# A first projection by Strassen's identity in a hybrid decoder layer, with every engine's instructions in program order

## The chip, the cores and the metric

The kernel runs on one core of one Trainium2 chip. The metric is the time of one execution in microseconds (us) of device time. Of the kernel before there are three timed runs, with a median of 2120.15 us (2118.58 to 2121.61), and one profiled execution.

## What is computed

The layer takes x of 1024 tokens by 2048, all in float32. It normalises x, scales and shifts it by a modulation computed from c, and projects the result h to 8192 columns. These hold eight quantities of eight heads with 128 columns each: q, k, v, z of a stick-breaking attention, and q, k, v, z of a retention. The two groups' outputs are gated with SiLU(z), joined, projected back with `w_out`, gated and added to x.

```python
mod = silu(c) @ w_ada + b_ada
shift, scale, gate = split(mod, 3)
h = rms_norm(x, norm_gain) * (1.0 + scale) + shift          # 1024 x 2048
proj = h @ w_in                                             # 2048 x 8192, the "first projection"
q_sb, k_sb, v_sb, z_sb, q_r, k_r, v_r, z_r = split(proj)    # 1024 columns each, 8 heads of 128
qa, ka = rms_norm(q_sb, sb_q_gain), rms_norm(k_sb, sb_k_gain)          # per head
# stick-breaking, per head: z = qa.ka / sqrt(128); for s < t
#   A[t,s] = sigmoid(z[t,s]) * prod_{s<j<t} (1 - sigmoid(z[t,j]));  oa = A @ v
oa = stick_breaking_attention(qa, ka, v_sb) * silu(z_sb)
# retention, per head: o_t = sum_{s<=t} gamma^(t-s) (q_t.k_s) v_s, in chunks of 128 with a state
ob = head_group_norm(chunkwise_retention(rotary(q_r), rotary(k_r) / sqrt(128), v_r)) * silu(z_r)
y = concat(oa, ob) @ w_out                                  # 2048 x 2048, the "second projection"
return x + gate * y
```

## The kernel before

**Numbers and products.** Every large product is made in a split form: a float32 operand is cut into a high part and a low part (both in the type fp32r), and three matmuls, high by high, high by low and low by high, are added up in PSUM. `mm3` (L130 to L134) issues the three. A weight tile that has arrived from memory is cut by `split_w`: ScalarE (ACT) copies the high part (`wh`, L118), and VectorE (DVE) subtracts it to get the low part (`wl`, L120). The activations h are kept whole on chip for the entire first projection, 16 row chunks of 128 by two token halves of 512, as `h_hi` and `h_lo`.

**First projection.** Two helpers compute it. `unit_t` makes one head of one quantity transposed (128 columns by 512 tokens): the weights are the stationary operand, h is the moving one. `unit_v` makes two heads of v with the tokens on the partitions: h is stationary and 256 columns of weights move.

```python
def unit_t(col0, halves, name, lo_pool=()):          # 16 chunks x 2 halves x 3 matmuls of 512 columns
    ...
            mm3(o[hf], hi[:, sl], lo[:, sl], h_hi[kc, hf], h_lo[kc, hf], kc == 0, kc == KC - 1)
def unit_v(col0, name):                              # 16 chunks x 8 token blocks x 3 matmuls of 256 columns
    ...
            mm3(o[tb // 2][:, (tb % 2) * 256:(tb % 2) * 256 + 256],
                h_hi[kc, tb // 4][:, tk], h_lo[kc, tb // 4][:, tk], hi[:, sl], lo[:, sl], ...)
```

**Stages.** (1) Start: x is loaded, normalised and turned; the modulation is summed from `w_ada` chunk by chunk (`ada_sums`, two-pass float32 matmuls `accp`, L282); meanwhile the z columns of seven retention heads are computed for the first token half, as chunks of h become ready (`first`), before the shift is known. Then the other token half of these columns, while the shift is summed and added to h (`shift_h`, L318 to L323); the missing share of the shift is added to z later (`z_bias`). (2) For each stick-breaking head: q, k, z by `unit_t`, and for every second head v by `unit_v`. In between, the attention of the head before is issued piece by piece. (3) The same for the retention heads. (4) The second projection, in output columns of 512: first the two token halves of the first columns (`y_0a`, `y_0b`), then three units with all eight token blocks (`y`).

**Order.** TensorE (PE) runs in the order in which the program issues: after every six matmuls of a projection, `tick` lets one waiting task (a generator such as `sb_attention`, `ret_attention`, `qk_norm`, `gate_parts`) issue its next piece. The other engines' order is chosen by the tile layer's scheduler, with some steps raised by `high_priority`. Buffers are tags of tile pools.

**Queries and keys.** `qk_norm` squares q and k on GpSimd (POOL), averages over the head by a matmul with a constant matrix (`ms`, L545 and L546), and takes the inverse root on tiles of 128x512 by three Newton steps on ACT and DVE (L553 to L555). z and v of a head go to memory (`zsb`, `vraw`) and come back when the attention needs them.

**End.** `finish` (L944 to L948) loads a tile of x (`xr`), multiplies the projection's tile by the gate, adds x, and stores.

Of the kernel before, what the change touches and what calls it, by code (L numbers as in the profile page):

```python
# [11 lines left out]
F32 = mybir.dt.float32  # L12
# [5 lines left out]
P = 128  # L18
S = 1024
# [11 lines left out]
NORM_GAP = 3  # L31
NORM_GAP2 = 6
SPLIT_GAP = 2
ZT = 1
BE = 3
TURN = 2
TURN_PRIO = 400
RT_ONE = False
ZB_GAP = 2
K0_WAIT = 8  # L40
NZ = 7
ADA_BUFS = 9
SHIFT_GAP = 6
X_LOAD = {3: (4,), 5: (5,), 7: (6,), 8: (7,)}
X_STAT = {5: (4,), 7: (5,), 9: (6,), 10: (7,)}
X_TURN = 10
MOD_AT = 4
ENG = mybir.EngineType
MANUAL = (ENG.PE,)
LO_POOL = ()  # L50
RT_GAP = 5
# [3 lines left out]
def layer_kernel(ctx, tc, x, c, w_ada, b_ada, norm_gain, w_in, sb_q_gain, sb_k_gain, ret_norm_gain, w_out,  # L55
# [7 lines left out]
    hp = ctx.enter_context(tc.tile_pool(name="hp", bufs=1))  # L63
    wp = ctx.enter_context(tc.tile_pool(name="wp", bufs=3))
    ps = ctx.enter_context(tc.tile_pool(name="ps", bufs=1, space=PS))
    dr = ctx.enter_context(tc.tile_pool(name="dr", bufs=1, space=bass.MemoryType.DRAM))

    concat = [dr.tile([P, S], F32, name=f"concat{f}") for f in range(KC)]
    gate_row = dr.tile([1, D], F32, name="gate_row")

# [5 lines left out]
    mean_r = cons.tile([P, P], F32R, name="mean_r")  # L76
    nc.vector.memset(mean_r.bitcast(F32), 1.0 / HD)

    c_sb = hp.tile([P, HALF], F32, tag="hl14_1", name="c_sb")[:, 0:16]
# [9 lines left out]
    rows = hp.tile([P, HALF], F32, tag="hl15_1", name="rows")  # L89
# [8 lines left out]
    nc.vector.tensor_copy(cols, rows_ps[:, 0:58])  # L98
    gain_c = cols[:, 0:16]
    shift_b = cols[:, 16:32]  # L100
    qg = cons.tile([P, 1], F32, name="qg")
    nc.vector.tensor_scalar(qg, cols[:, 48:49], 1.0 / math.sqrt(HD), None, op0=ALU.mult)
    kg = cols[:, 49:50]
# [9 lines left out]


    def split_w(raw, name, lo_eng=nc.vector):
        n = raw.shape[1]
        hi = wp.tile([P, HALF], F32R, tag="wh", name=f"wh_{name}")
        nc.scalar.activation(hi[:, 0:n], raw, AF.Copy)  # L118
        lo = wp.tile([P, HALF], F32R, tag="wl", name=f"wl_{name}")
        lo_eng.tensor_tensor(lo[:, 0:n], raw, hi[:, 0:n].bitcast(F32), op=ALU.subtract)  # L120
        return hi, lo

    def wchunk(parts, name, lo_eng=nc.vector):
        raw = wp.tile([P, HALF], F32, tag="wr", bufs=3, name=f"wr_{name}")
        for dst, src in parts(raw):
            nc.sync.dma_start(dst, src)
        return split_w(raw, name, lo_eng)

    w_in_k = w_in[0].rearrange("(k p) n -> p k n", p=P)

    def mm3(o, a_hi, a_lo, b_hi, b_lo, first, last):
        nc.tensor.matmul(o, a_hi, b_hi, start=first, stop=False)  # L132
        nc.tensor.matmul(o, a_hi, b_lo, start=False, stop=False)  # L133
        nc.tensor.matmul(o, a_lo, b_hi, start=False, stop=last)  # L134
# [3 lines left out]
    def unit_t(col0, halves, name, lo_pool=()):  # L138

        o = {hf: ps.tile([P, HALF], F32, tag="pj", bufs=4, name=f"pj_{name}_{hf}") for hf in halves}  # L140
        for kq in range(4):
            def parts(raw):
                yield raw.rearrange("p (k n) -> p k n", n=P), w_in_k[:, 4 * kq:4 * kq + 4, col0:col0 + P]
            with tc.high_priority(AHEAD):
                hi, lo = wchunk(parts, f"{name}_{kq}", nc.gpsimd if kq in lo_pool else nc.vector)
            for hf in halves:
                for k in range(4):
                    kc = 4 * kq + k
                    sl = slice(k * P, (k + 1) * P)
                    mm3(o[hf], hi[:, sl], lo[:, sl], h_hi[kc, hf], h_lo[kc, hf], kc == 0, kc == KC - 1)  # L150
                    if k % 2:
                        yield
        return o

    def unit_v(col0, name):

        o = [ps.tile([P, HALF], F32, tag="pj", bufs=4, name=f"pv_{name}_{b}") for b in range(4)]
        for kk in range(8):
            def parts(raw):
                yield raw.rearrange("p (k n) -> p k n", n=2 * P), w_in_k[:, 2 * kk:2 * kk + 2, col0:col0 + 2 * P]  # L160
            with tc.high_priority(AHEAD):
                hi, lo = wchunk(parts, f"{name}_{kk}")
            for tb in range(NB):
                for k in range(2):
                    kc = 2 * kk + k
                    sl = slice(k * 2 * P, (k + 1) * 2 * P)
                    tk = slice(tb % 4 * P, (tb % 4 + 1) * P)
                    mm3(o[tb // 2][:, (tb % 2) * 256:(tb % 2) * 256 + 256],
                        h_hi[kc, tb // 4][:, tk], h_lo[kc, tb // 4][:, tk], hi[:, sl], lo[:, sl],
                        kc == 0 and tb % 2 == 0, kc == KC - 1 and tb % 2 == 1)  # L170
                if tb % 2:
                    yield
        return o
# [3 lines left out]
    tasks = []  # L177
    one_step = [True]

    def tick():  # L180
        stepped = False
        for task in list(tasks):
            task[1] -= 1
            if task[1] > 0 or stepped and one_step[0]:
                continue
            stepped = True
            try:
                task[1] = next(task[0])
            except StopIteration:
                tasks.remove(task)  # L190

# [3 lines left out]
    def steady(unit):  # L195
        while True:
            try:
                next(unit)
            except StopIteration as e:
                return e.value  # L200
            tick()

    def drain():
        while tasks:
            tick()
# [5 lines left out]
    zcol = 7 * GW  # L211
    zraw = [dr.tile([P, S], F32, name=f"zraw{h}") for h in range(NZ)]
    shift = cons.tile([P, KC], F32, name="shift")
    zsb = [dr.tile([P, S], F32, name=f"zsb{h}") for h in range(NH)]
    vraw = [dr.tile([P, NB, 2, P], F32, name=f"vraw{i}") for i in range(NH // 2)]
    zb = cons.tile([P, 8], F32, name="zb")
    with tc.tile_pool(name="st", bufs=1) as st:
        xt, ada, xT = {}, {}, {}

        def load_x(t):  # L220
            for qt in range(4):
                xt[t, qt] = hp.tile([P, HALF], F32, tag=f"hh{4 * qt + t % 4}_{t // 4}", name=f"x_{t}_{qt}")
                nc.sync.dma_start(xt[t, qt], x2[t * P:(t + 1) * P, qt * HALF:(qt + 1) * HALF])

        def load_ada(cc, gs=range(4)):

            col = (D if cc < 8 else 0) + (cc % 8) * 2 * P
            for g in gs:
                ada[cc, g] = ar = st.tile([P, 4, 2 * P], F32, tag="ada", bufs=ADA_BUFS, name=f"ada_{cc}_{g}")
                nc.sync.dma_start(ar, ada_rows[:, 4 * g:4 * g + 4, col:col + 2 * P])  # L230

        def half_tile(name):
            return st.tile([P, HALF], F32, tag="ht", bufs=3, name=name)

        def x_squares(ts):
            ss = st.tile([P, 2, 4], F32, tag="ss", bufs=2, name=f"ss_{ts[0]}")
            for i, t in enumerate(ts):
                for qt in range(4):
                    junk = half_tile(f"junk_{t}_{qt}")
                    nc.scalar.activation(junk, xt[t, qt], AF.Square, accum_out=ss[:, i, qt:qt + 1])  # L240
            return ss

        def x_scale(ts, ss):

            n = len(ts)
            nc.vector.tensor_tensor(ss[:, 0:n, 0:2], ss[:, 0:n, 0:2], ss[:, 0:n, 2:4], op=ALU.add)
            m = st.tile([P, 2], F32, tag="m", bufs=2, name=f"m_{ts[0]}")
            nc.vector.tensor_tensor(m[:, 0:n], ss[:, 0:n, 0], ss[:, 0:n, 1], op=ALU.add)
            nc.vector.tensor_scalar(m[:, 0:n], m[:, 0:n], 1.0 / D, EPS, op0=ALU.mult, op1=ALU.add)
            y = st.tile([P, 2], F32, tag="y", bufs=2, name=f"y_{ts[0]}")  # L250
            u = st.tile([P, 2], F32, tag="u", bufs=2, name=f"u_{ts[0]}")
            rsqrt_newton(y[:, 0:n], m[:, 0:n], u[:, 0:n])
            for qt in range(4):
                for i, t in enumerate(ts):
                    if i % 2:
                        nc.scalar.activation(xt[t, qt], xt[t, qt], AF.Copy, scale=y[:, i:i + 1])
                    else:
                        nc.vector.tensor_scalar(xt[t, qt], xt[t, qt], y[:, i:i + 1], None, op0=ALU.mult)

        def x_turn(kc, g, tag, bufs):  # L260

            xT[kc, g] = hp.tile([P, HALF], F32, tag=f"hl{kc}_{g}", name=f"xT{kc}_{g}")
            tp = ps.tile([P, HALF], F32, tag=tag, bufs=bufs, name=f"xtp_{kc}_{g}")
            for t in range(4):
                src = xt[4 * g + t, kc // 4]
                nc.tensor.transpose(tp[:, t * P:(t + 1) * P], src[:, (kc % 4) * P:(kc % 4 + 1) * P], ident)
# [93 lines left out]
        for t in range(4):  # L360
            load_x(t)
# [644 lines left out]
```

## Time and profile before

| | before |
|---|---|
| median of three runs | 2120.15 us |
| the profiled execution: its time, its span | 2122.75 us, 2120.8 us |
| PE / DVE / ACT / POOL busy | 2074.5 / 1117.3 / 701.1 / 202.0 us |
| granted PE clock, mean | 0.999 |
| moved by DMA | 224.31 MB, 106 GB/s on average |

The profile's page gives the busy time of each engine, the same in 40 slices of the span (a digit is tenths), the chain of work that ended last, and groups of instructions. Matmuls overlap each other in the records: a record is longer than the distance to the next one, so costs of matmuls are taken from the distance of their starts. A two-pass float32 matmul (operands not in fp32r) has two records; a transpose has one. SP is the engine that issues nearly all DMA transfers, in order, on one queue.

### The profile page before, as it was taken

The numbers are of one execution on the slowest core, as the hardware profiler recorded it, in microseconds if no ns is written. First come the engines' busy times: TensorE is split into PE (matmuls) and PEld (weight loads), VectorE is DVE, ScalarE is ACT, GpSimd is POOL, SyncE is SP. The second block draws the span as 40 slices with busy tenths as digits, with TensorE's granted clock in tenths as the row PEclk, the third lists the DMA queues.
The fourth block names the chain that finished last, engine by engine and source line by source line (L and its number), as shares of the span: only waits on it lengthen the run. The fifth ranks groups of instructions, "written<-read, shape, count | busy, mean of one in ns | idle before, by whom it ended". The sixth has DMA issues, their size and how long they took to land.

```text
span 2120.8 us, 30239 instructions
## 1 busy us (share of the span) xinstructions
PE 2074.5 (98%) x11679; PEld 1771.8 (84%) x11679; DVE 1117.3 (53%) x2165; ACT 701.1 (33%) x1312; POOL 202.0 (10%) x342
## 2 busy tenths in 40 slices
PE   5999999999999999999999999999999999999998
PEld 4777789888988898889888888988989988688887
DVE  4664662768166826783575556466354156513132
ACT  5453442544244514442453232222122223311110
POOL 0000000111021102110211112011011010000000
PEclk9999999999999999999999999999999999999999
DMA  9977212121212122211222533333332125624132
GB/s 293 335 253 226 85 60 75 46 70 60 80 46 70 45 75 66 70 45 55 85 70 87 175 101 113 110 92 102 101 91 63 50 73 167 215 90 134 48 126 79
DMA packets 232403, 224.31 MB, mean 106 GB/s; under 512 B 12674, under 2 KB 187844, under 8 KB 232260
## 3 DMA queue, kind: packets, MB, share of 16 engines
q1 hardware_dynamic: 231872, 222.36, 33.2%
q8 instruction: 91, 1.49, 0.3%
q14 instruction: 52, 0.43, 0.1%
q10 hardware_dynamic: 388, 0.04, 0.0%
HBM read 194.03 MB, written 28.32 MB: 105 GB/s over the span
## 4 chain that ended last, share of the span: by engine, by line
PE 83%; DVE 8%; DMA 5%; ACT 3%; issue 2%; POOL 0%; SPq 0%; ACTq 0%; DVEq 0%; POOLq 0%
PE y L132 4%; PE y L133 4%; PE y L134 4%; PE pv_v L134 3%; PE pv_v L133 3%; PE pv_v L132 3%; PE pj_rq L132 3%; PE pj_rq L134 3%; PE pj_rq L133 3%; PE pj_q L133 3%; PE pj_rk L132 3%; PE pj_rk L134 3%; PE pj_rk L133 3%; PE pj_q L134 3%; PE pj_q L132 3%; PE pj_z L132 2%
## 5 line engine op out<-in xcount | busy, mean ns | idle before, releaser
L132 PE MATMUL y<-wh_o,c_hi 128*128 128x512 f32 x384 | 149.4, 389 | 0.0
L133 PE MATMUL y<-wl_o,c_hi 128*128 128x512 f32 x384 | 149.4, 389 | 0.0
L134 PE MATMUL y<-wh_o,c_lo 128*128 128x512 f32 x384 | 149.4, 389 | 0.0
L132 PE MATMUL pv_rv<-wh_rv,h_hi 128*128 128x256 f32 x512 | 145.8, 285 | 3.4 <-ACT wh_rv L118 3.4
L133 PE MATMUL pv_rv<-wl_rv,h_hi 128*128 128x256 f32 x512 | 145.3, 284 | 1.8 <-DVE wl_rv L120 1.8
L133 PE MATMUL pv_v<-wl_v,h_hi 128*128 128x256 f32 x512 | 144.9, 283 | 0.0
L132 PE MATMUL pv_v<-wh_v,h_hi 128*128 128x256 f32 x512 | 144.9, 283 | 0.0
L134 PE MATMUL pv_v<-wh_v,h_lo 128*128 128x256 f32 x480 | 135.8, 283 | 0.0
L134 PE MATMUL pv_rv<-wh_rv,h_lo 128*128 128x256 f32 x480 | 135.8, 283 | 0.0
L120 DVE TENSOR_TENSOR wl_o<-wr_o,wh_o 128x512 fp32r<-128x512 f32 x48 | 33.2, 692 | 181.7 <-ACT wh_o L118 181.7
L627 DVE TENSOR_TENSOR_SCAN om<-om 128x128 f32<-128x128 f32 (+2 forms) x96 | 96.3, 1003 | 43.5 <-POOL om L617 42.2
L118 ACT ACTIVATE wh_o<-wr_o 128x512 fp32r<-128x512 f32 x48 | 30.3, 632 | 220.7 <-PE y L134 216.3
L132 PE MATMUL pj_rq<-h_hi,wh_rq 128*128 128x512 f32 x256 | 102.6, 401 | 0.0
L132 PE MATMUL pj_rk<-h_hi,wh_rk 128*128 128x512 f32 x256 | 102.3, 400 | 0.0
L132 PEld LDWEIGHTS pv_rv<-wh_rv,h_hi 128*128 128x128 f32 x512 | 98.2, 192 | 4.9 <-ACT wh_rv L118 4.0
L132 PE MATMUL pj_z<-h_hi,wh_z 128*128 128x512 f32 x256 | 101.3, 396 | 0.0
L133 PEld LDWEIGHTS pv_rv<-wl_rv,h_hi 128*128 128x128 f32 x512 | 98.2, 192 | 2.7 <-DVE wl_rv L120 2.6
L132 PE MATMUL pj_k<-h_hi,wh_k 128*128 128x512 f32 x256 | 100.3, 392 | 0.0
L132 PE MATMUL pj_q<-h_hi,wh_q 128*128 128x512 f32 x256 | 100.1, 391 | 0.0
L134 PE MATMUL pj_rq<-h_hi,wl_rq 128*128 128x512 f32 x256 | 100.0, 391 | 0.0
L134 PE MATMUL pj_rk<-h_hi,wl_rk 128*128 128x512 f32 x256 | 99.9, 390 | 0.0
L134 PE MATMUL pj_q<-h_hi,wl_q 128*128 128x512 f32 x256 | 99.9, 390 | 0.0
(270 smaller groups left out, 5520.3 us busy)
## 6 DMA issues: line engine op xcount, KB each, us to landing
ada<-in_w_ada_dram SPq DMA_DIRECT2D x64, 512.0 KB
gr<-in_w_ada_dram SPq DMA_DIRECT2D x64, 256.0 KB
wr_o<-in_w_out_dram SPq DMA_DIRECT2D x48, 256.0 KB
x<-in_x_dram SPq DMA_DIRECT2D x32, 256.0 KB
wr_rz<-in_w_in_dram SPq DMA_DIRECT2D x32, 256.0 KB
wr_q<-in_w_in_dram SPq DMA_DIRECT2D x32, 256.0 KB
wr_k<-in_w_in_dram SPq DMA_DIRECT2D x32, 256.0 KB
wr_z<-in_w_in_dram SPq DMA_DIRECT2D x32, 256.0 KB
```

Source lines behind the costliest of these rows:

```text
L118: nc.scalar.activation(hi[:, 0:n], raw, AF.Copy)
L120: lo_eng.tensor_tensor(lo[:, 0:n], raw, hi[:, 0:n].bitcast(F32), op=ALU.subtract)
L132: nc.tensor.matmul(o, a_hi, b_hi, start=first, stop=False)
L133: nc.tensor.matmul(o, a_hi, b_lo, start=False, stop=False)
L134: nc.tensor.matmul(o, a_lo, b_hi, start=False, stop=last)
L627: nc.vector.tensor_tensor_scan(rev, rev, rev, init, op0=ALU.mult, op1=ALU.bypass)
```

## The change

**Strassen's identity.** The first projection is done as a block product of two by two: columns of `w_in` in pairs of heads, rows in two halves of 1024 (A11, A12, A21, A22, each 128 columns by 1024 rows), and h in two row halves by two token halves (B11 to B22). Seven products of half size replace eight. On the side of h the seven right factors (B11, B21, B22 and the combinations T1 to T4) are made once, cut into high and low parts, and stored in memory (`fac`, 56 pairs of 256 KB tiles). On the side of the weights the sums and differences are made by DVE on the arrived tiles (`one_sum`, and one subtraction in `left`). Three of the four results accumulate over several products in PSUM and are read in between; the rest is added by DVE (`evac`).

**Groups.** 56 pairs of heads' columns make seven groups of four pairs. A group runs seven products, each over two row quarters (`hh`) and four pairs (`q`): an entry is four chunks, twelve matmuls of 512 columns. For each entry the weights are loaded, summed and cut three entries ahead (`LOOK`), and the right factors come from memory through 24 slots (`ring`). There are 400 entries.

**Plain first.** The columns computed first and without Strassen are now the queries of seven retention heads (both token halves, 672 matmuls of 512); the eighth head's queries ride along in group 0. While the second token half runs, the shift is summed, the right factors are made (`factors`) and mostly stored.

**v and the others.** v is computed transposed like the rest and turned by PE when the attention needs it (`turn_v`, `values_in`); `unit_v` is gone. Every result of a group except the retention z goes to memory (`proj`) and is read back. `qk_norm` is replaced by `prepare`: squares on ACT, sums by `nm` (a two-pass float32 matmul with 32 columns of ones), roots on tiles of 128x16, the inverse root of q as the scale of the two sigmoids, that of k as a row read back on all partitions.

**Order and buffers.** From the second plain pass on, all engines run in program order (`tc.manual_schedule()` without a list). Steps that need another engine's result are issued some ticks later (`later(n, ...)`). All large tiles are 92 slots of 128x512 given out by hand (`Slots`), from a certain point on in classes (14 for results, 24 for raw weights, 24 for the ring, 30 for attention).

**The second projection** keeps its matmuls. The retention z is gated there (`cut_step`), six of the eight gate parts are summed there (`gate_steps`), and the x tiles are loaded two token blocks ahead (`load_xr`).

The core of the diff:

```diff
-ctx.enter_context(tc.manual_schedule(engines={mybir.EngineType.PE}))
+ctx.enter_context(tc.manual_schedule())
...
+KCS = (0, 1, 8, 9, 2, 3, 10, 11, 4, 5, 12, 13, 6, 7, 14, 15)
+RIGHT = {1: "B11", 2: "B21", 3: "B22", 4: "T4", 5: "T1", 6: "T2", 7: "T3"}
+ORDER = (4, 1, 6, 5, 3, 2, 7)
+FRESH = (4, 1, 2, 7)
...
+    for a in range(0, NH, 2):
+        groups.append([(base + a * P, proj[f"{n}{a}"], proj[f"{n}{a + 1}"])
+                       for n, base in (("q", 0), ("k", GW), ("z", 3 * GW), ("v", 2 * GW))])
+    for a in (0, 4):
+        groups.append([(base + b * P, proj[f"{n}{b}"], proj[f"{n}{b + 1}"])
+                       for b in (a, a + 2) for n, base in (("rk", 5 * GW), ("rv", 6 * GW))])
+    groups.append([(7 * GW + a * P, a, a + 1) for a in range(0, NH, 2)])
...
+    def pump():
+        while ring_list and len(slots.free["ring"]) >= 2:
+            gi, prod, kc = ring_list.popleft()
+            n = RIGHT[prod]
+            hi = get(f"{n}h_{gi}_{kc}", "ring", F32R)
+            nc.sync.dma_start(hi.bitcast(F32), fac[n, kc][:, 0])
+            lo = get(f"{n}l_{gi}_{kc}", "ring", F32R)
+            nc.sync.dma_start(lo.bitcast(F32), fac[n, kc][:, 1])
+            ring[gi, prod, kc] = hi, lo
+        n = 2
+        while pumping[0] is True and raw_list and slots.free["raw"] and n:
+            load_raw(*raw_list.popleft())
+            n -= 1
...
+    def one_sum(gi, hh, q, n):
+        r = {b: raws[gi, q, b, hh] for b in ("A11", "A21", "A22")}
+        o, a, b = {1: ("A22", "A22", "A21"), 3: ("A21", "A11", "A21"), 2: ("A11", "A22", "A11")}[n]
+        nc.vector.tensor_tensor(r[o], r[a], r[b], op=ALU.add if n == 1 else ALU.subtract)
...
+    def evac(gi, prod, q, o):
+        def copy(cc):
+            dst[q, cc] = t = get(f"c{cc}_{gi}_{q}", "dst", borrow=gi == LAST)
+            nc.scalar.activation(t, o, AF.Copy)
+        def add(cc):
+            nc.vector.tensor_tensor(dst[q, cc], o, dst[q, cc], op=ALU.add)
...
+    def run_entry(j):
+        gi, prod, hh, q = entries[j]
+        prepare_entry(j + LOOK)
+        if q == 0:
+            for k in range(4):
+                rts[k] = right(gi, prod, 4 * hh + k)
...
+        for k in range(4):
+            sl = slice(k * P, (k + 1) * P)
+            mm3(bank[q], hi[:, sl], lo[:, sl], rts[k][0], rts[k][1], fresh and k == 0, hh == 1 and k == 3, True)
+            if last_q:
+                put(*rts.pop(k))
+            if k == 3 and hh:
+                later(1, lambda: evac(gi, prod, q, o))
+            if k % 2:
+                tick()
...
-    def unit_v(col0, name):
-    def qk_norm(r, gain, pool, name):
+    def prepare(h):
+            nc.tensor.matmul(nm[32 * g:32 * g + 32, 256 * i:256 * i + 256], ones, ...)
```

As built, the instructions change so (counted in the two programs):

| | before | after |
|---|---|---|
| matmuls of 512 columns in the first projection | 4608 | 5472 |
| matmuls of 256 columns in the first projection | 3072 | 0 |
| matmuls of 512 columns in the second projection | 1536 | 1536 |
| matmuls with the constant matrix (`ms`, 512 columns) | 64 | 0 |
| `nm` matmuls, 256 columns, two-pass | 0 | 64 |
| transposes of v and in `prepare` | 0 | 168 |
| DVE / ACT / POOL instructions | 2167 / 1289 / 347 | 2583 / 1378 / 283 |
| DMA transfers, MB | 786, 222 | 1916, 486 |

1724 lines of the change are left out of this document (1043 added, 681 removed).

## The prediction

> **What bounds the kernel now.** I read the page first: busy shares, the 40 slices, the chain.
>
> ```profile
> span 2120.8 us, 30239 instructions
> ...
> PE 2074.5 (98%) x11679; PEld 1771.8 (84%) x11679; DVE 1117.3 (53%) x2165; ACT 701.1 (33%) x1312; POOL 202.0 (10%) x342
> ...
> PE   5999999999999999999999999999999999999998
> ...
> PEclk9999999999999999999999999999999999999999
> DMA  9977212121212122211222533333332125624132
> ...
> q1 hardware_dynamic: 231872, 222.36, 33.2%
> ...
> PE 83%; DVE 8%; DMA 5%; ACT 3%; issue 2%; POOL 0%; SPq 0%; ACTq 0%; DVEq 0%; POOLq 0%
> ```
>
> PE is busy in all slices but the first and is 83% of the chain; the clock is full. But overlapping records make a PE busy that is only slow, so I asked the view of waits what PE waited for (columns: total us, times, longest).
>
> ```profile
> PE accp L282 <- DVE ss L246: 11.0, 1, 11.0
> PE rows_ps L97 <- DMA rows<-in_ret_norm_gain_dram: 8.8, 1, 8.8
> PE pv_rv L132 <- ACT wh_rv L118: 3.4, 3, 2.4
> PE ms_k L545 <- ACT be L615: 3.2, 7, 0.6
> ```
>
> Two waits of the start make 20 us; everything after it is a few us per cause. So the kernel is bound by the number of PE's matmuls, and the question is how many fall away, and whether what replaces them (transfers, DVE sums) stays hidden.
>
> **Prices of PE.** From the timeline, starts (first column) of equal matmuls in a row:
>
> ```profile
> 1930.11 0.39 PE L133 MATMUL y<-wl_o,c_hi 128*128 128x512 f32 x1
> 1935.55 0.39 PE L133 MATMUL y<-wl_o,c_hi 128*128 128x512 f32 x1
> 560.08 0.28 PE L133 MATMUL pv_v<-wl_v,h_hi 128*128 128x256 f32 x1
> 571.00 0.28 PE L134 MATMUL pv_v<-wh_v,h_lo 128*128 128x256 f32 x1
> 28.85 1.95 PE L266 MATMUL xtp<-ident,x 128*128 128x128 f32 x16
> L282 PE MATMUL accp<-ada,silu_z 128*32 128x256 f32 x512 | 33.3, 398 | 12.8 <-DVE ss L246 11.0 <-DMA ada<-in_w_ada_dram 1.1 <-DVE xT L268 0.7
> ```
>
> The two 512-column starts lie 24 matmuls apart: 5.44/24 = 0.227 us each. The 256-column ones lie 91 apart: 10.92/91 = 0.120, so two of them cost 0.240 where one wide one costs 0.227. Sixteen turns take 1.95 us with the last one's length in it: about 0.11 each. The two-pass sums (`accp`) take 33.3/512 = 0.065 a record. All are costs per instruction on the path, since PE hardly waits.
>
> **The sum, against the profiled execution's 2122.75 us** (span 2120.8 and 1.95 around it; 2.6 above the median of the runs, 0.12%).
>
> 1. The 3072 matmuls of `unit_v` go: 3072 x 0.120 = -368.6. The 512-column ones of the first projection go from 4608 to 5472: 864 x 0.227 = +196.1. Net -172.5. Of this, 672 x 0.227 = 152.5 is Strassen's and the rest is v computed wide. Accumulating in PSUM across products adds no matmul.
> 2. `qk_norm`'s `ms` goes: 64 x 0.227 = -14.5. `nm` comes: 64 of two records, 128 x 0.065 = +8.3. 168 turns come: x 0.11 = +18.5. Net +12.3.
> 3. The tail. The chain before ends on a load of x that waited behind PE's end:
>
> ```profile
> 2110.70 0.24 PE y L134
> 2112.41 0.34 SPq L948
> ...
> 2112.81 4.12 DMA xr<-in_x_dram
> ...
> 2117.02 0.69 DVE yt L947
> ```
>
> `load_xr` asks for it two token blocks earlier, so -4 (bounds -4 and 0).
>
> This gives 2122.75 - 172.5 + 12.3 - 4 = 1958.5 if nothing new waits. What could (operations and bytes by stage are counted in the program as built, in its order):
>
> 4. **Transfers.** They grow from 222 to 486 MB. The first matmul of the first projection starts here:
>
> ```profile
> 31.66 0.50 PE L132 MATMUL first<-h_hi,wh_first 128*128 128x512 f32 x1 [0.86 <-ACT h_hi L308]
> ```
>
> With PE's time by the prices above:
>
> | stage | MB | PE us | GB/s asked |
> |---|---|---|---|
> | start and two plain passes | 70 | 32 to that matmul + 200 | 303 |
> | group 0 | 56 | 176 | 321 |
> | groups 1 to 6, each | 49 to 53 | 183 to 198 | 257 to 283 |
> | second projection, first unit | 25 | 90 | 280 |
> | its last three units | 32 | 262 | 122 |
>
> What the engines can move shows where they are full, in the view of windows (last columns: PE clock, DMA share, GB/s):
>
> ```profile
> 0.00:100.00 100.00, 77.98 (x529) 57.46 (x530) 54.77 (x174) 51.30 (x118) 0.70 (x6) 1.00 0.97 323
> 100.00:200.00 100.00, 98.56 (x666) 76.42 (x665) 57.23 (x99) 44.74 (x76) 0.00 (x0) 1.00 0.79 253
> 60.00:100.00 40.00, 40.00 (x251) 30.52 (x250) 26.42 (x93) 17.08 (x42) 0.00 (x0) 1.00 1.05 365
> 1760.00:1868.00 108.00, 104.17 (x457) 82.34 (x456) 60.59 (x125) 35.36 (x57) 1.29 (x1) 0.98 0.62 201
> ```
>
> At a share of 0.97 they moved 323, at best 365; 253 at 0.79 and 201 at 0.62 scale to about 320 full. So groups 1 to 6 ask 80 to 88% of a full rate of 320 or 70 to 78% of 365, with factors asked for two blocks of four entries (20 us and more) ahead: hidden. Up to the end of group 0 it is tight: 126 MB need 391 us at 323 and 346 at 365, beside PE's 32 + 376 = 408. The mean fits; the order within need not, since the store of a factor must end before its slot is loaded again. I take +8, between 0 and +40 (a tenth of the 391). Issuing costs 0.34 of SP's time each (the store above): 1911 x 0.34 = 650 us of some 1980, hidden.
>
> 5. **DVE.** Its 512-element operation costs
>
> ```profile
> L120 DVE TENSOR_TENSOR wl_o<-wr_o,wh_o 128x512 fp32r<-128x512 f32 x48 | 33.2, 692 | 181.7 <-ACT wh_o L118 181.7
> L491 DVE SCALAR_TENSOR_TENSOR ga<-gr,silu_c,ga 128x256 f32<-128x256 f32 x120 | 63.0, 525 | 18.3 <-DMA gr<-in_w_ada_dram 15.8
> 239.56 0.75 DVE L318 SCALAR_TENSOR_TENSOR h<-h_hi,shift,h_lo 128x512 f32<-128x512 f32 x1
> 240.22 0.69 DVE L323 TENSOR_TENSOR h_lo<-h,h_hi 128x512 fp32r<-128x512 f32 x1
> 240.83 0.75 DVE L318 SCALAR_TENSOR_TENSOR h<-h_hi,shift,h_lo 128x512 f32<-128x512 f32 x1
> ```
>
> 0.69 us as a record, and 0.61 to 0.66 from start to start in a dense row. In groups 1 to 5 it has 140 to 150 such operations and 40 to 45 us of small ones: 136 to 147 us beside 183 to 191 of PE, hidden; ACT has 59 to 99 there and POOL less than before. Not hidden are two places. In the second plain pass and the opening of group 0 (weights, bias of the queries, h, and the factors at once) it has 115 operations of 512 and 37 smaller: about 100 us beside 100 of PE, and PE's next entries wait for its `wl`. I take +4 (0 to +12). In the first unit of the second projection it has 116 x 0.69 + 49 x 0.525 = 106 us beside 90: the cuts of the joined outputs, the gating with z moved here, and the gate's sums. By the dense pitch it is 95 to 100. I take +8 (0 to +16).
>
> 6. **Waits from program order.** On DVE, a sum or an `evac` that waits for PE's last matmul of an entry now stands ahead of later `wl` in a fixed queue; PE's entry three further on, 3 x 12 x 0.227 = 8 us later, waits for these. SP's stores stand ahead of factor loads in the same way, covered by the 20 us. With these leads I take what PE already waits now from its third row on, about as much again: +8 (0 to +90, below).
>
> Forecast: 1958.5 + 8 + 4 + 8 + 8 = **1986**; its own range, 1963 to 2015, adds the smaller bounds of 4 to 6.
>
> **Rivals.**
>
> *Nothing new waits: 1958* (1945 to 1963). For it: in groups 1 to 6 no engine is asked for more than PE gives it time for, and the leads of 8 and 20 us exceed the 4.12 us of the load above. Against it: stages at 95 to 100% of a second engine.
>
> *Fixed order costs each block: 2046* (2015 to 2118). A group has 14 blocks (7 products by two row quarters), in all 98; if at each one PE waits about 0.9 us for a `wl` held up behind an `evac`, that is 88 us on 1958. For it: such waits exist already (`pv_rv` for `wh_rv` up to 2.4 us) where DVE and ACT are only half busy. Against it: leads of three entries.
>
> The window of 1760 to 1868 above has PE waits and a clock of 0.98, 2 us lost in 108. [...] No row here shows waits that long outside the start, so this is 1 in 100.
>
> *Transfers become the bound: slower than before.* All go through SP's one queue, and as built eight completion semaphores are used in turn, so a ninth transfer waits for the first. Taking out the last units (262 us, 32 MB) and 22 us at the ends, 454 MB must pass in 2123 - 284 = 1839 us to break even: 247 GB/s. Below that the change loses; at 230 the time is 1974 + 284 = 2258. For it: the run's mean is 106 and no stretch longer than 100 us is over 323; with 512-byte rows in the weights and stores among loads the rate could drop. Against it: the 253 of the second window came at a share of 0.79, so it was the pace asked, not the limit.
>
> The row of 60 to 100 us moved 365 GB/s in transfers of 256 and 512 KB. [...] I give the slower side from transfers 10 in 100.
>
> *The change does not do what it says*: the built program has the 5472 matmuls, so no chance worth a number.
>
> **How the numbers follow.** Forecast 62, nothing waits 12, fixed order 14, slower 11 (10 and 1), no change 1, of 100. What a measurement of this kernel can tell from no change is about 0.2%, 4 us: faster 0.88, same 0.01, slower 0.11. The range takes the first two cases whole and most of the third: 1950 to 2085, leaving out some 3 below and 15 above.
>
> **What would show it.** Right: PE's records about 9,700 (5472 + 1536 wide ones), no slice under 9 but the first, DMA digits of 7 to 9 up to the first unit of the second projection, some 486 MB, DVE near 1300 us; PE's waits of 20 us at the start, then DVE `wl` near 200 us and in the first unit. Wrong: PE digits of 7 or 8 through groups 1 to 6, waits of PE on ring tiles (`T1h`, `B11h`) or on `wl` at every block, a clock under 0.98.

## The result and the profile after

| | before | after |
|---|---|---|
| median of four runs each, same chip | 2120.88 us (2118.58 to 2121.61) | 2053.27 us (2050.84 to 2056.50) |
| ratio of the times | 1 | 0.968, 95% interval 0.967 to 0.970 |
| profiled execution: time, span | 2122.75, 2120.8 us | 2056.50, 2054.8 us |
| granted PE clock, mean | 0.999 | 0.989 |

The change is faster by 67.6 us. The forecast was 135 us faster (1986), so the direction and the range (1950 to 2085) held, and half of the gain did not come. The rest of this document is about the 67 us between 1986 and 2053. One of the four runs of an experiment below (v's load six ticks earlier) took 10989.55 us, so its time is the median of the other three and its trace is not used.

From the page of the kernel after: span, busy times, and the 40 slices of PE, of its clock and of the DMA engines.

```profile
span 2054.8 us, 28414 instructions
...
PE 1944.9 (95%) x9703; PEld 1578.5 (77%) x9703; DVE 1276.4 (62%) x2581; ACT 761.5 (37%) x1401; POOL 81.1 (4%) x278
...
PE   5998899999999999998999999999998998899998
...
PEclk9999899999999999999999999999999999999999
DMA  9967798987686678776866786999987567654041
...
q1 hardware_dynamic: 381194, 485.65, 72.4%
```

9703 records and 485.65 MB are what was forecast, DVE's 1276 us too. New against before are the eights in PE's row: the fourth and fifth slice (154 to 257 us, the second plain pass), single ones later, and a pair at 1695 to 1798 (the second projection's first units). PE has holes there. The view of waits names them (total us, times, longest):

```profile
PE accp L523 <- DVE xT L508: 13.1, 5, 3.2
PE y L186 <- ACT ch L1353: 12.9, 10, 3.0
...
PE zp L186 <- DVE vl L951: 8.0, 6, 1.5
PE otp L1225 <- DVE on L1217: 7.6, 4, 4.2
PE vtp L945 <- DMA vr<-pr_v: 7.4, 4, 2.7
PE zp L186 <- ACT nr L865: 4.7, 4, 1.9
PE rvt L1145 <- DMA rv<-pr_rv: 4.4, 3, 1.8
...
PE pj L187 <- DVE B21l L586: 2.2, 1, 2.2
```

No cause is large, and of those shown only the last, once 2.2 us, is a projection's entry (`pj`) waiting, there for a factor. What waits is not the projection but what is issued between its entries: the modulation's sums (`accp`), v's turns (`vtp`, `rvt`), scores (`zp`), the retention's outputs (`otp`); and, at the end, the first two units of `y`.

To place the loss I put the matmuls of each trace beside the program's order, priced each as in the prediction (0.227, 0.120, 0.11, 0.065 us, and 0.175 for 384 columns), and took for each stage the time from its first matmul's start to that of the next stage, less the priced sum: the time **lost over price**. (The 9 to 10 us ahead of the first matmul of all and the 6 us behind the last one are in no row.)

| us lost over price | before | after |
|---|---|---|
| start, to the first projected matmul | 16.8 | 14.4 |
| the columns done plain (two passes) | 4.0 | 25.3 (1.7 and 23.6) |
| group 0 | | 3.6 |
| groups 1 to 6 (before: the heads) | 32.5 | 83.2 |
| second projection | 11.8 | 32.0 |
| sum | 65.1 | 158.5 |
| priced matmuls, whole kernel | 2041.0 | 1880.3 |

The matmuls are 160.7 us cheaper, as forecast (-172.5 + 12.3 = -160.2). About 93 us came back as holes, where the forecast allowed 28.

**How one hole is made.** In the second plain pass the turned x (`xtp`) leaves PE at 165.7 us and must be copied (`xT`, L508) before PE may write the same PSUM bank again as `accp`. From the timeline of after (start, duration, engine, line, operation), PE first, then DVE:

```profile
165.04 0.66 PE L503 MATMUL xtp<-ident,x 128*128 128x128 f32 x4 [0.28 <-DVE shift L546]
...
170.96 1.93 PE L523 MATMUL accp<-ada,silu_z 128*32 128x256 f32 x32 [3.21 <-DVE xT L508]
```

```profile
165.56 0.68 DVE L573 TENSOR_TENSOR T<-xT,xT 128x512 f32<-128x512 f32 x1
166.16 0.68 DVE L573 TENSOR_TENSOR T<-xT,T 128x512 f32<-128x512 f32 x1
166.76 0.68 DVE L586 TENSOR_TENSOR B21l<-xT,B21h 128x512 fp32r<-128x512 f32 x1
167.36 0.68 DVE L586 TENSOR_TENSOR T1l<-T,T1h 128x512 fp32r<-128x512 f32 x1
167.97 1.15 DVE L175 TENSOR_TENSOR wl_first<-wr,wh_first 128x512 fp32r<-128x512 f32 x2
169.04 1.27 DVE L715 SCALAR_TENSOR_TENSOR qb_acc<-wr,shift,qb_acc 128x512 f32<-128x512 f32 x2
170.23 0.68 DVE L508 COPY xT<-xtp 128x512 f32<-128x512 f32 x1
```

From 165.7 on, the factors (`T`, `B21l`, `T1l`), two weight cuts and two bias sums stand ahead of the one copy that PE needs next. DVE is doing useful work all the while, in the wrong order for PE. PE stands still for 3.21 us. A load does the same on ACT. For the gate of z in the attention, ACT's place for the sigmoid is fixed three ticks after the load is issued; the view of ACT's waits says:

```profile
ACT sg L1043 <- DMA zr<-pr_z: 47.9, 16, 5.1
```

Sixteen times ACT stops for 3.0 us on average, and whatever is queued behind it on ACT is held up by as much.

### The profile page after: what moved, and what is told of

It is laid out like the page before. It is cut to its first block, busy times and chain, and to the rows that moved or that the text cites. A ratio compares the mean times of both kernels' runs of the same rounds, so it can differ in the third digit from the quotient of the medians.

```text
span 2054.8 us, 28414 instructions
## 1 busy us (share of the span) xinstructions
PE 1944.9 (95%) x9703; PEld 1578.5 (77%) x9703; DVE 1276.4 (62%) x2581; ACT 761.5 (37%) x1401; POOL 81.1 (4%) x278
## 3 DMA queue, kind: packets, MB, share of 16 engines
q1 hardware_dynamic: 381194, 485.65, 72.4%
## 4 chain that ended last, share of the span: by engine, by line
PE 69%; DVE 13%; DMA 11%; ACT 3%; issue 3%; SPq 1%; DVEq 0%; ACTq 0%
PE pj L186 13%; PE pj L187 13%; PE pj L188 13%; PE y L186 4%; PE y L187 4%; PE y L188 4%; PE first L186 2%; PE first L187 2%; PE first L188 2%; DMA zr<-pr_z 2%; DVE wl L175 1%; DMA gr<-in_w_ada_dram 1%; PE accp L523 1%; DMA vr<-pr_v 1%; DVE om L983 1%
## 5 line engine op out<-in xcount | busy, mean ns | idle before, releaser
L175 DVE TENSOR_TENSOR wl<-A,wh 128x512 fp32r<-128x512 f32 x400 | 274.4, 688 | 306.7 <-ACT wh L173 277.1
L173 ACT ACTIVATE wh<-A 128x512 fp32r<-128x512 f32 x400 | 251.1, 629 | 458.3 <-PE pj L187 357.6
L186 PE MATMUL y<-wh_o,ch 128*128 128x512 f32 x512 | 203.8, 398 | 12.9 <-ACT ch L1353 12.9
L187 PE MATMUL y<-wl_o,ch 128*128 128x512 f32 x512 | 202.1, 395 | 3.1 <-DVE wl_o L175 3.1
L188 PE MATMUL y<-wh_o,cl 128*128 128x512 f32 x512 | 202.6, 396 | 0.1
L186 PEld LDWEIGHTS y<-wh_o,ch 128*128 128x128 f32 x512 | 97.5, 190 | 38.2 <-ACT ch L1353 17.8
L292 DVE TENSOR_TENSOR A<-A,A 128x512 f32<-128x512 f32 x168 | 113.8, 686 | 9.9 <-DMA A<-in_w_in_dram 8.1
L188 PEld LDWEIGHTS y<-wh_o,cl 128*128 128x128 f32 x512 | 97.4, 190 | 25.7 <-DVE cl L1354 5.6
L187 PEld LDWEIGHTS y<-wl_o,ch 128*128 128x128 f32 x512 | 97.7, 191 | 23.7 <-DVE wl_o L175 3.9
L186 PE MATMUL pj<-T1h,wh 128*128 128x512 f32 x232 | 93.9, 405 | 0.0
```

The costliest lines, as they stand in the source:

```text
L173: nc.scalar.activation(hi[:, 0:n], src[:, 0:n], AF.Copy)
L175: nc.vector.tensor_tensor(lo[:, 0:n], src[:, 0:n], hi[:, 0:n].bitcast(F32), op=ALU.subtract)
L186: nc.tensor.matmul(o, a_hi, b_hi, start=first, stop=False, skip_group_check=on)
L187: nc.tensor.matmul(o, a_hi, b_lo, start=False, stop=False, skip_group_check=on)
L188: nc.tensor.matmul(o, a_lo, b_hi, start=False, stop=last, skip_group_check=on)
L292: nc.vector.tensor_tensor(r[o], r[a], r[b], op=ALU.add if n == 1 else ALU.subtract)
```

## The experiments

Three theories were tried against each other: **order** (pieces stand in the wrong place of a fixed queue, so what PE needs is late although the engines have time), **amount** (DVE has too much to do) and **transfers** (485 MB are too much). A time is the median of four runs unless said otherwise, with the ratio to before on the same chip and its interval; the changed kernel is 2053.27 us, 0.968. The experiments ran on several chips, on which the kernel before took 2120.9 to 2123.2 us, and the intervals are about 3 us either way, so a difference of two times below that is under some 5 us is not clear of noise.

### One hole at a time

*x's copy in the second plain pass, from DVE to ACT.*

```diff
-        if p % 2:
+        if p % 2 and g == 0:
             nc.vector.tensor_copy(xT[kc, g], tp)
```

> In the second plain pass PE lost 23.6 us, half of it where the modulation's sums wait for the PSUM bank that the copy of the turned x on VectorE releases. Here these copies are all made by ScalarE. Order theory (the bank is released late because the copy stands behind the factors' work in VectorE's fixed queue): that wait and the half clock it causes go, the pass shrinks from 123.6 to 102 to 108 us, the whole by 15 to 21 us. Occupancy theory (VectorE has too much work there): 7 copies of 0.69 us move, so at most 5 us. Transfer theory (the DMA engines are full up to the end of group 0): within 4 us of no change.

2055.92 us, 0.969 (0.967 to 0.971): no gain. In its trace the wait for DVE's `xT` is gone and the pass loses 16.1 us over price in place of 23.6, but other waits have come up: `accp` for ACT's `xT` (3.5 us), `xtp` for DVE's `shift` (3.3 for 0.8), and at the opening of group 0, which loses 7.1 for 3.6, `pj` for `wl` (2.5) and ACT's `zt` (1.8). So about half of what the pass gained was lost again at the next place in the fixed queues. The rest went in the unit `y1` (17.4 for 13.5) and group 6 (24.5 for 22.5), far from this edit; runs whose edits change nothing there either lose 15 to 16 and 23 to 25. Neither the 15 to 21 us of the order theory nor the pass of 102 to 108 us (it took 116) came.

*z's gate in the second projection, one chunk ahead.* `gate_z(i + 1)` issues the removed lines for the next chunk after this chunk's cut, so that ACT no longer waits for DVE between `zsg` and `ch`.

```diff
             t = craw.pop((f, half))
-            if f >= NH:
-                z = zkeep.pop((f - NH, half))
-                sg = anywhere(f"zsg_{f}_{half}")
-                nc.scalar.activation(sg, z, AF.Sigmoid)
-                nc.vector.tensor_tensor(z, z, sg, op=ALU.mult)
-                nc.vector.tensor_tensor(t, t, z, op=ALU.mult)
-                put(z, sg)
             hi, lo = anywhere(f"ch_{f}_{half}", F32R), anywhere(f"cl_{f}_{half}", F32R)
...
             c_hi[f, half], c_lo[f, half] = hi, lo
+            gate_z(i + 1)
...
```

> The gating of the retention outputs with SiLU(z) is issued one chunk earlier, behind the cut of the chunk before, with the same instructions. Order theory (ScalarE's cut of the joined outputs waits for a chain ScalarE, VectorE, VectorE and holds up the next weights' cut): the first unit of the second projection shrinks from 120 us to 104 to 108, the whole by 12 to 16. Occupancy theory (VectorE's 106 us of work bound that unit): not below 106, at most 14 and likely under 6, since its work is unchanged. Transfer theory: no change.

2041.97 us, 0.9625 (0.961 to 0.964): 11 us, just under the 12 to 16 expected. The wait of `y` for `ch` falls from 12.9 to 3.0 us, the two units lose 18.9 in place of 30.1, and a wait of 6.1 us for `wl_o` is left.

*v's load six ticks earlier,* and *v's turned copy in another PSUM bank* (A1 in place of A0, which scores and norms share):

```diff
+        vr = {hf: load_v(hf) for hf in range(2)}
         for hf in range(2):
             qt.append(get(f"q_{h}_{hf}", "att"))
...
-            if s == 0:
-                vr = {hf: load_v(hf) for hf in range(2)}
...
```
```diff
-            tp = ps.tile([P, HALF], F32, tag="A0", name=f"vtp_{h}_{hf}")
+            tp = ps.tile([P, HALF], F32, tag="A1", name=f"vtp_{h}_{hf}")
```

> v of a stick-breaking head is asked for six ticks earlier. Transfer theory in its mild form (a load under traffic takes 5 us and more, longer than its five ticks): the waits of the turns of v for that load (7.4 us in all) go, 5 to 8 us less. Order theory: the wait only moves to the next step, within 4 us of no change.

> The turned v uses the PSUM bank A1, which is free then, and no longer A0, which the scores need a tick later. Order theory (short leads on a shared bank): the scores' waits for the low part of v (8.0 us in all) go, 5 to 8 us less. Transfer and occupancy theories: no change.

The early load alone: 2057.31 us over three runs, 0.970 (0.968 to 0.972), nothing. The bank alone: 2045.11 us, 0.9645 (0.963 to 0.966), 8 us; the wait of `zp` for `vl` is gone, and the longest one in the groups is then v's load, 8.1 us in four.

*The last three together:*

> Three edits together: z's gate one chunk ahead (alone -11 us), v's turned copy in the PSUM bank A1 (alone -8 us) and v loaded six ticks earlier (alone nothing). After the bank was changed, TensorE's longest wait in the groups was the one for v's load (8.1 us in four). If leads in series hide one another (the load shows only when the bank is free), the three give 11 + 8 + 5 to 8, about 2026 to 2030 us; if the early load is worth nothing in any case, 2034.

2028.47 us, 0.9555 (0.954 to 0.957), as expected: 25 us, 5 more than the gate and the bank give alone (11 and 8). PE's waits for `vl` and for `vr` are both gone from its list. That fits leads in series, of which the one that ends last hides the others, so that the early load shows only once the bank is free; but 5 us are of the size of the noise (the four runs lie between 2023.65 and 2033.71), so the load's share is not shown by the time alone.

### Amount and transfers

*168 sums of weight blocks left out* (the products take unsummed blocks):

```diff
-        nc.vector.tensor_tensor(r[o], r[a], r[b], op=ALU.add if n == 1 else ALU.subtract)
```

> The 168 sums of weight blocks on VectorE (about 116 us of its 1276) are left out, so that Strassen's products take unsummed blocks; all else stays. If VectorE's amount of work is what holds TensorE back in groups 0 to 6, 25 us or more go, nearly all of them between 256 and 1665 us of the span. If it is the lead of single copies and their place in the order, 5 to 12 us go there, and the second plain pass (23.6 us over its matmuls) and the first two units of the second projection (30 us over) stay within 3 us of what they were.

```profile
PE 1945.3 (95%) x9703; PEld 1578.5 (77%) x9703; DVE 1175.5 (57%) x2413; ACT 761.7 (37%) x1401; POOL 82.1 (4%) x278
```

2052.47 us, 0.966 (0.965 to 0.968). A hundred us of DVE's work are gone and the time is the same within the noise (the intervals of the two ratios overlap); groups 1 to 6 lose 82.5 over price, for 83.2. So the amount of work on DVE was no cause of the groups' holes. The 5 to 12 us that the order theory expected there did not come either.

*The ring loads high parts only* (the low part is left out of the products and the high part stands in):

```diff
-            lo = get(f"{n}l_{gi}_{kc}", "ring", F32R)
-            nc.sync.dma_start(lo.bitcast(F32), fac[n, kc][:, 1])
-            ring[gi, prod, kc] = hi, lo
+            ring[gi, prod, kc] = hi, hi
...
```

> The ring of Strassen's factors loads only their high parts (the low parts are left out of the product, the high part standing in for them), so about 130 MB of the 486 MB are gone and no matmul. If the added time is the price of the transfers (rival: transfers become bound), 25 us or more go, and PE's waits on loads (x, ada, vr, rv: 21 us together) fall by half. If it is short leads in a fixed order, on copies and shared PSUM banks, the time falls by 0 to 6 us, what the waits of vtp for vr (7.4 us) give, and the waits on DVE and ACT stay as they were.

2027.12 us, 0.9546 (0.953 to 0.956): 26 us. Moved were 391.26 MB, so 94 MB fewer and not 130. By the expectation this time speaks for transfers, against the order theory. Groups 1 to 6 lose 52.1 in place of 83.2; the waits for `vr` fall from 7.4 to 2.3 us, ACT's for `zr` from 47.9 to 13.8. The other signs were the order theory's: PE's waits for `xT` (13.0), `ch` (12.8) and `vl` (8.0) stayed, and so did the two loads of the start (18.7). But a late load and a fixed order can't be told apart here; that needs the same cut in a free order (below).

### The order itself

*The one line that fixes all engines.* PE keeps its order; that of the others is chosen by the scheduler.

```diff
-    ctx.enter_context(tc.manual_schedule())
```

> The instruction that fixes every engine to the program's order is taken out; PE's order is still fixed, the others' is chosen by the scheduler, as in the kernel before. If the program's order of VectorE and ScalarE makes the stalls (copies that TensorE needs next stand behind sums, factor openings and gates), the time falls by 15 to 40 us and the waits of accp for xT (13 us) and of y for ch (13 us) go. If TensorE would meet the same short leads whatever the order behind it, it stays within 8 us of the changed kernel or grows, since a scheduler that goes by its own estimate of the times puts other work in front of them.

1972.82 us, 0.929 (0.927 to 0.930): 80 us, twice what was expected at most. The same matmuls, sums and bytes. Page and waits of this kernel:

```profile
PE 1922.8 (98%) x9703; PEld 1579.6 (80%) x9703; DVE 1256.1 (64%) x2581; ACT 766.6 (39%) x1401; POOL 101.0 (5%) x278
...
PE   5999999999999999999999999999999989999999
...
DMA  9979998886887689768976899899987676825131
```

```profile
PE otp L1224 <- DVE on L1216: 12.9, 5, 3.7
...
PE rvt L1144 <- DVE on L1216: 7.7, 3, 2.9
PE pj L188 <- DVE wl L175: 1.3, 1, 1.3
```

One eight is left, and beside the start only the retention's norm holds PE for long (20.6 us); the other waits are 1.3 us or less each. The second plain pass, in the windows (columns: us, then busy us of PE, PEld, DVE, ACT, POOL; clock, DMA share, GB/s), first after, then this kernel:

```profile
132.10:255.70 123.60, 109.68 (x650) 81.05 (x649) 91.75 (x162) 72.37 (x126) 0.00 (x0) 0.93 0.78 259
```
```profile
132.00:233.30 101.30, 101.30 (x649) 78.11 (x648) 91.19 (x162) 79.11 (x133) 0.00 (x0) 1.00 0.97 319
```

The same 162 DVE operations and 91 us of them, 22 us less time, the clock whole, and the DMA engines at 97% without a hole in PE.

*Half of the ring's loads again, in the free order:*

> The scheduler's order and, in it, half of the ring's traffic (the low parts of the right factors are left out, the high part stands in). In the fixed order this half was worth 26 us. If the transfers cost time of their own, it is worth 15 us or more here too (1958 or less from 1973). If they cost only through the fixed order, a late load holding what is queued behind it, it is worth 0 to 5 us (1968 to 1973), and TensorE's waits on the retention's norm (20 us) stay.

```profile
q1 hardware_dynamic: 329354, 391.26, 62.6%
```

1971.91 us, 0.929 (0.9275 to 0.931): nothing, where it gave 26 us in the fixed order, and the waits on the norm stay (`otp` 13.2, `rvt` 8.2). So these 94 MB have no price of their own once the order is free. In the fixed order they cost by making loads late that have a fixed place in SP's queue, with their users at a fixed place behind them.

*One queue released at a time.* `manual_schedule` takes a list of engines; all but the released ones were listed (SP is not in this list), and the others keep their order instruction for instruction.

```diff
-    ctx.enter_context(tc.manual_schedule())
+    ctx.enter_context(tc.manual_schedule(engines={mybir.EngineType.PE, mybir.EngineType.DVE, mybir.EngineType.Activation, mybir.EngineType.Pool}))
```

> SyncE alone is released from the program's order; PE, VectorE, ScalarE and GpSimd keep it instruction for instruction. Theory A, copies stand behind other work on VectorE and ScalarE: within 10 us of the changed kernel's 2053. Theory B, loads stand behind stores that wait on SyncE's queue, and a load that comes late holds the engine that is to use it and all that is queued behind: 25 us or more go (the 26 that halving the ring's loads gave), all of it in groups 1 to 6, and ScalarE's wait for z's load (48 us in 16 times in groups 1 to 5) falls below 20.

> ScalarE alone is released from the program's order. Theory A: its waits for a load of z (48 us) and for VectorE's sums no longer stand in front of copies that TensorE needs, so 15 to 40 us go, in groups 1 to 6 and in the first two units of the second projection; the second plain pass, where the copy that is late stands on VectorE, stays at 20 or more over its matmuls. Theory B: within 10 us.

> VectorE alone is released from the program's order. Theory A: the second plain pass loses its 20 us (the copy xT no longer stands behind factors and bias sums), the wait of vl (8 us) goes, together 20 to 40 us; groups 1 to 6 otherwise keep what stands on ScalarE. Theory B: within 10 us in groups 1 to 6.

> SyncE and VectorE released from the program's order, ScalarE, GpSimd and PE keep it. Alone the two gave 38 and 41 us; all four gave 80. If each order has stalls of its own, the two together give 70 to 80 (1974 to 1983) and ScalarE's order costs nothing beside them. If the orders hold one another up (a copy on ScalarE waits for VectorE's sum, which waits for a load), they give 55 to 65 (1988 to 1998), and ScalarE's release, 20 alone, is worth 15 to 25 still.

| released | us | ratio | plain passes | groups 0 to 6 | second projection |
|---|---|---|---|---|---|
| none (after) | 2053.27 | 0.968 (0.967 to 0.970) | 25.3 | 86.8 | 32.0 |
| ACT | 2033.78 | 0.958 (0.957 to 0.960) | 12.3 | 73.9 | 33.8 |
| SP | 2015.49 | 0.950 (0.948 to 0.952) | 23.2 | 51.2 | 29.8 |
| DVE | 2012.25 | 0.947 (0.945 to 0.949) | 14.0 | 63.3 | 24.1 |
| SP and DVE | 1987.11 | 0.936 (0.935 to 0.938) | 17.2 | 34.5 | 21.2 |
| all but PE | 1972.82 | 0.929 (0.927 to 0.930) | 3.0 | 44.3 | 14.4 |

(The last three columns are us lost over price.) Both theories that had been set against each other are right, in different places: SP's release took 36 us out of the groups and little elsewhere; DVE's took 11 out of the plain passes, 8 out of the second projection and 23 out of the groups; ACT's took 13 out of the plain passes and 13 out of the groups. Two of these went against the expectations. With ACT released the second plain pass was to stay at 20 us or more over price, and fell from 23.6 to 10.6 (PE's wait of `accp` for `xT` from 13.1 to 7.1). With DVE released the whole 20 us were to go there and little in the groups; about 11 went there, and 23 in the groups. Alone ACT, SP and DVE give 19, 38 and 41 us, 98 in sum, and 80 together, so about a fifth is shared. I read this as holes that either of two releases would close; no run shows which. The pair came at 1987, between its two expected ranges. Releasing ACT and POOL as well is worth 14 more: the plain passes gain 14 and the second projection 7, while the groups lose 10, all of it in group 6.

What SP's release does shows in v's loads (duration ns, first and last start). First the group of loads in after, with its waiter:

```profile
L939 SPq DMA_DIRECT2D vr<-pr_v x16: 319/430/677, 483.1 to 1196.3; - x16
...
  PE vtp L945: 7.4, 4
```

Then the same loads with SP free:

```profile
L939 SPq DMA_DIRECT2D vr<-pr_v x16: 319/320/499, 381.1 to 1157.7; - x16
...
L945 PE MATMUL vtp<-ident,vr x64: 270/272/273, 491.2 to 1188.6; 128*128 128x128 f32 x64
```

The first load goes at 381.1 us for a turn at 491.2, where in the fixed order it went at 483.1, some 10 us ahead of its use; no one waits for `vr` any more, and ACT's 47.9 us for `zr` are gone from its list. In after the first head's stores are issued at 340.0 and 413.7 us, 143 and 69 us ahead of that load; only its place in the program kept the load back.

### What is left in the free order

*Two edits there, then a priority:* the retention's pieces of head 4 three ticks apart like those of heads 0 to 3, with the bank of the run above; and the norm's operations on DVE ahead of other work.

```diff
-    ctx.enter_context(tc.manual_schedule())
-            for i, wait in enumerate(ret_attention(h, r, RT_GAP if h < 4 else RT_GAP2)):
+            for i, wait in enumerate(ret_attention(h, r, RT_GAP if h < 5 else RT_GAP2)):
-            tp = ps.tile([P, HALF], F32, tag="A0", name=f"vtp_{h}_{hf}")
+            tp = ps.tile([P, HALF], F32, tag="A1", name=f"vtp_{h}_{hf}")
```
```diff
+NORM_PRIO = 300
...
-            later(1, norm)
+            def norm_first():
+                with tc.high_priority(NORM_PRIO):
+                    norm()
+            later(1, norm_first)
```

> The scheduler's order for all engines but PE, and two edits on what was left there: the pieces of retention heads 0 to 4 (not 0 to 3) issued three ticks apart, and v's turned copy in bank A1. With the scheduler's order alone TensorE still waited 20.6 us for VectorE's norm of the retention (otp and rvt), nearly all in group 6 and the opening of the second projection. If those are short leads, a wider gap for one head of the last four takes 3 to 8 us; the bank, worth 8 us in the fixed order, is worth under 2 here, where zp waited 0.8 us for vl. So about 1965; if the heads' end only moves into the second projection, 1973.

> The kernel with the scheduler's order, the wider gap and the bank, and the retention's norm on VectorE given a higher priority than other work. TensorE waits there 16 us for the norm (otp 10.6, rvt 5.5). If the norm only stands behind cuts and sums, 8 to 14 us go (1948 to 1954 from 1962); if its own chain of some 25 small operations is as long as the lead, nothing changes (1962 within 4).

1961.79 us, 0.924 (0.922 to 0.925), a little better than expected; and 1957.72 us, 0.923 (0.9215 to 0.924), the lowest of all: 163 us under before and 96 under the change as made. What the priority gave, 4 us by the medians, is not clear of noise (the two intervals overlap), and it is less than the 8 to 14 expected; its waits are

```profile
PE otp L1228 <- DVE on L1217: 10.1, 4, 4.9
...
PE rvt L1145 <- DVE on L1217: 5.0, 3, 3.6
```

against 10.6 and 5.5 without it. So the norm's place in DVE's queue is hardly what is left. Either its own chain of small operations is too long or the lead is too short; which of them stays open.

## Why the prediction was right and wrong

**Steps 1 and 2, the matmuls: right.** Priced over the trace, they are 160.7 us cheaper, forecast 160.2. The prices from distances of starts carried over.

**Step 3, the tail (-4): about 0.** From the end of PE's last matmul to the end of the span it is 5.7 us, 5.8 before. DVE waits for a load of `xr` once near the end, for 1.02 us just ahead of the last three matmuls, and for none after; its own products on the last tiles and the last store fill the same six microseconds.

**Step 4, transfers (+8): 0 by themselves.** Group 0, which was called tight, lost 3.6 us, and 1.7 in the free order. The stated reason why transfers would be hidden held. The factors, asked for 20 us ahead, were there in time (no wait for a load of theirs is in PE's list). What the step missed is that every hidden transfer needs a request that is early enough: the loads of v and z, asked for some 10 and 4 us ahead, were not.

**Step 5, DVE (+4 and +8): the holes were there, the reason was not.** The second plain pass lost 20 us more than the plain passes before, the first two units of the second projection 18 more (30.1 against 11.8). Both were put down to DVE's amount of work against PE's. But with the same operations in a free order the two places lose 1.3 and 12.5 us, about what they lost before. The cover that was doubted, DVE's time, was sufficient; the order was not. Nor was it `wl`, as forecast, that held PE there (`wl_o` 3.1 us), but the copies `xT` and `ch`, 13 us each.

**Step 6, waits from program order (+8): this is the step that failed.** It measured 80 us, the gap between the fixed and the free order. The step looked for waits of the projection's entries on `wl` and on stores ahead of factor loads, found leads of 8 and 20 us, and took "what PE already waits now, about as much again". Those leads did hold: PE's list of waits has `wl` of the first projection once, with 0.7 us. What was never costed are the short leads of everything else in the queues: pieces issued one to four ticks (1.4 to 5.4 us) ahead of their use, behind whatever the program puts there. The before kernel had the scheduler for that, so its waits were no measure of a fixed order. They were also misread: from the third row on that view sums to 19.6 us, not 8. And the range of 1963 to 2015 can't be had from the bounds of steps 4 to 6, which leave 1958 to 2116.

**The rivals.** "Fixed order costs each block, 2046" had the cause in general and nearly the time (2053), but the nearness is luck: its mechanism, PE waiting at each of 98 blocks for a `wl` held up behind an `evac`, is not in the trace. At 14 in 100 it was too low: the diff takes the scheduler away from four engines at once, and that deserved its own range. "Nothing new waits, 1958" is what the kernel does once the order is freed and three small edits are made on it (1957.7); that it agrees within 1 us is partly chance, since the tail did not shrink and 15 us of new waits on the norm are left, offset elsewhere. "Transfers become the bound" is refuted by the free order: all 486 MB pass beside a PE that is busy for 98%. Of the 11 in 100 for a slower kernel, 1 was for a slow clock; no run shows a cost per wait that would give that. Measured were 44 us at a clock of 0.50 in the changed kernel, whose matmuls took some 19 us over their price.

The sums close: 1958.5 of the prediction, 4 for the tail that did not shrink, and the 10 that groups 1 to 6 lose there more than the heads did before (42.6 against 32.5, mostly the retention's norm) give the 1973 of the free order, and 80 more for the fixed one give the 2053 measured.

## What to carry to other kernels

An order written by hand must be costed as an edit of its own: list every piece whose result PE takes within a few microseconds, and see what stands ahead of it on each queue, loads on SP included. Busy shares and bandwidth don't show this: with DVE at 62% and the DMA engines at 72%, the fixed order cost 80 us, and taking 100 us of work from DVE changed nothing that could be measured. To tell order from amount, release one engine's order at a time with all work unchanged; and repeat a test of traffic in the free order, since in a fixed one a late load looks like a lack of bandwidth (94 MB less gave 26 us in the fixed order here, and nothing in the free one).

## What the runs showed of the hardware

A hole can cost more than its length. The clock of the changed kernel falls to 0.50 for short stretches. In after (windows as above):

```profile
183.29:186.70 3.41, 1.19 (x12) 0.61 (x14) 3.41 (x7) 0.69 (x2) 0.00 (x0) 1.00 1.05 394
186.70:190.12 3.42, 3.42 (x34) 1.59 (x22) 2.43 (x5) 0.30 (x1) 0.00 (x0) 0.50 1.00 342
190.12:193.53 3.41, 3.41 (x18) 2.83 (x17) 1.71 (x3) 1.38 (x3) 0.00 (x0) 1.00 1.04 359
```

PE is busy for 1.19 of the first 3.41 us, and the next 3.42 us run at half the clock. Such stretches start at 186.7, 203.8, 237.9, 790.9, 1203.9, 1548.6, 1668.1, 1719.3 and 1777.3 us and last 3.4 or 6.8 us each: 44 us in all, whose matmuls took some 19 us over their price. In the free order it is 27 us, and 12 over, so by these numbers the clock makes some 7 of the 80 us. Not every hole has such a stretch behind it: after the stall of 3.21 us at 167.8 the clock stays at 1.00 up to 186.7. What decides between the two is not shown.
